# The output gate of the modulation: summed by columns during attention and spread through DRAM, instead of summed by rows late and spread by TensorE

## The chip, the cores and the metric

The kernel runs on one core of a Trainium2 chip. The metric is the device time of one execution in microseconds, and of several executions the median is taken.

## What is computed

A layer of an encoder: 512 tokens of 1024 channels, one conditioning vector `c`. Cut to what matters here:

```python
mod = jax.nn.silu(c) @ w_c[l] + b_c[l]                 # 1024 -> 3 * 1024
shift, scl, gate = jnp.split(mod, 3, axis=-1)
h = rms_norm(x, g_pre[l]) * (1.0 + scl) + shift
proj = h @ w_in[l]                                     # 1024 -> 8 * 1024
xa, za, q, k, v, zb, ga, gb = jnp.split(proj, split_pts, axis=-1)
y_a = (recurrence over xa) * silu(za) @ w_pa[l]
y_b = (neighbourhood attention of q, k, v) * silu(zb) @ w_pb[l]
merged = sigmoid(ga) * y_a + sigmoid(gb) * y_b
x = x + gate * (merged @ w_o[l])
return rms_norm(x, g_final)
```

`shift` and `scl` are needed at the start, `gate` (1024 numbers, the last third of `mod`) only near the end, where it multiplies the output of the product with `w_o`. The kernel multiplies it into the columns of `w_o` instead, so it needs `gate` as a row, the same on all 128 partitions.

## The kernel before, in words

All matrix products are made of float32 in three passes: each operand is split into a rounded part (`hi`, by ACT) and the rest (`lo`, by DVE or POOL), and TensorE adds hi*hi, hi*lo and lo*hi. A projection (`proj`, L687 on) takes one block of 128 output channels: one load of 512 KB (`wraw`), one cast on ACT (`whi`), one subtraction of 128x1024 on DVE or POOL (`wlo`), and 24 matmuls of 128x512 into a bank of PSUM (`acc`).

The stages in order: the head (parameters, norm of x, modulation), the product for v (`hx`), then four groups of attention, each for two pairs of heads. In a group TensorE makes the six projections of the next group while the attention of the last one runs between them: scores (`sp`), on DVE the bias and the minimum of each row (L821, `p`, `mn`), on ACT the exponential, on TensorE the transposes (`pt`, L835), on ACT and DVE the hi and lo part of the transposed weights (`pp`, L841 and L843), on TensorE the product with v (`pv`), and on ACT and DVE its eviction (`vp` at L860 and L863, `yt` at L866). `pv` has two banks: a next `pv` can begin when `yt` of the one before has read its bank. Then come four groups of the recurrent branch, the merge of the two branches, and the product with `w_o`, followed by the final norm.

Each step is handed to `op` with an engine, an estimated cost and a rank. A planner (`Plan`) runs a list schedule at build time from these costs and writes out one fixed order for each engine. The engines then go through their rows in that order and wait for one another by semaphores. SP issues all loads and stores but two, in one order too. An op with `lock=True` on DVE is not planned beside one on POOL.

The gate is made late, in `gate_row` (L1084 to L1121), called after the recurrent groups. Sixteen loads of 256 KB bring the rows of the gate's third of `w_c` (`wr`). DVE multiplies each by the column `silc` (the silu of c, halved, L903) and adds them up in two tiles `g`, element by element (L1095, L1097). Each of the 128 partitions then holds a part of the sum. ACT and DVE split `g` into `gh` and `gl`, and TensorE multiplies both by a matrix of ones (`onesr`), which sums over the partitions and puts the row on all of them (`mi<-gh,onesr`, `mi<-gl,onesr`). DVE adds the bias from a broadcast load (L1113) and halves (L1115). `gate[n]` multiplies the columns of `w_o` (L1155).

`shift` and `scl` are made in another way, by columns (`modulate`, L539 on): a block of `w_c` comes turned, with 128 output channels on the partitions (`wc`), and one DVE instruction multiplies it by the row `silr` (silu of c on all partitions) and sums along the row (L569).

Of the kernel before, what the change touches and what calls it, by code (L numbers as in the profile page):

```python
# [331 lines left out]
@with_exitstack  # L332
def layer(ctx, tc, x, x_t, par, w_m, w_g, bc_gate, w_v, w_in, w_blk, rpb, amask, w_pa, w_pb, w_o, g_final, out):
    nc = tc.nc
# [56 lines left out]
    def whole(t):  # L391
        return lambda: t.ap


    def const(name, shape, dt=F32):
        return pl.fixed(cp.tile(shape, dt, name=name))

    ident, onesc, onesr = const("ident", [P, P]), const("onesc", [P, P]), const("onesr", [P, P], F32R)
    prm, silc, msk, par_sb = const("prm", [P, 120]), const("silc", [P, KD]), const("msk", [P, 80]), const("par_sb", [120, P])
    tan8 = const("tan8", [8, P])  # L400
# [11 lines left out]
    pp0 = B("mi")  # L412
    op("PE", 0.25, lambda e: nc.tensor.transpose(pp0.ap[:, :120], par_sb.ap, ident.ap[:120, :120]), -20,
       r=[par_sb, ident], w=[pp0])
    op("DVE", 0.3, lambda e: nc.vector.tensor_copy(prm.ap, pp0.ap[:, :120]), -20, r=[pp0], w=[prm])
    pc = lambda a, b: prm.ap[:, a:b]
# [13 lines left out]
    for n in range(2):  # L430
        cb = B("hx")

        def f(e, n=n, cb=cb):
            for k in range(4):
                nc.tensor.matmul(cb.ap[:, k * P:(k + 1) * P], ident.ap[:120, 4 * n + k:4 * n + k + 1].to_broadcast([120, P]), par_sb.ap,
                                 start=True, stop=True)
# [96 lines left out]
    def modulate(k):  # L533

        for m, d in ((1, scs), (0, shs)):
# [4 lines left out]
            if k == 0:  # L540
# [18 lines left out]
                continue  # L559
            load(t, whole(t), w_m[2 * k + m], k - 5, 524288, spare=2, name=f"wc{k}{m}")  # L560
            if k == 1:
# [336 lines left out]
    def small(rank, after):  # L898
# [185 lines left out]
    def gate_row(pos, after):  # L1084
        op("ACT", 0.3, lambda e: nc.scalar.copy(onesr.ap, onesc.ap), pos, r=[onesc], w=[onesr], after=after)
        g = (T("g"), T("g"))
        for kk in range(KD):
            for n in range(2):
                wr = T("wr")
                load(wr, whole(wr), w_g[kk * P:(kk + 1) * P, n * 512:(n + 1) * 512], pos + 0.5 * kk, 262144,  # L1090
                     after=after, spare=12, name="wr")

                def f(e, kk=kk, n=n, wr=wr):
                    if kk == 0:
                        nc.vector.tensor_scalar(g[n].ap, wr.ap, silc.ap[:, 0:1], None, op0=ALU.mult)  # L1095
                    else:
                        nc.vector.scalar_tensor_tensor(g[n].ap, wr.ap, silc.ap[:, kk:kk + 1], g[n].ap, op0=ALU.mult, op1=ALU.add)  # L1097
                op("DVE", dve(512), f, pos + 3 + 0.5 * kk, r=[wr, silc], **({"rw": [g[n]]} if kk else {"w": [g[n]]}), lock=True,
                   name="grow")
        for n in range(2):  # L1100
            gh, gl = T("gh", F32R), T("gl", F32R)
            op("ACT", act(512), cast(whole(gh), whole(g[n])), pos + 8, r=[g[n]], w=[gh])
            op("DVE", dve(512), sub(whole(gl), whole(g[n]), whole(gh)), pos + 8, r=[g[n], gh], w=[gl], lock=True)
            o, bcg, gf = B("mi"), T("gate"), T("gfin")

            def f(e, gh=gh, gl=gl, o=o):
                mm(o.ap, onesr.ap, gh.ap, True, False)
                mm(o.ap, onesr.ap, gl.ap, False, True)
            op("PE", 0.46, f, pos + 8, r=[onesr, gh, gl], w=[o], name="grow")
            load(bcg, whole(bcg), bc_gate[n * 512:(n + 1) * 512].partition_broadcast(P), pos + 7, 262144, after=after, spare=8)  # L1110

            def f(e, o=o, bcg=bcg):
                nc.vector.tensor_tensor(bcg.ap, o.ap, bcg.ap, op=ALU.add)  # L1113

                nc.vector.tensor_scalar(bcg.ap, bcg.ap, 0.5, None, op0=ALU.mult)  # L1115
            op("DVE", dve(512) + dve2(512), f, pos + 8.2, r=[o], rw=[bcg], lock=True, name="gate")
            gate.append(bcg)
# [202 lines left out]
```

## Time and profile before

| | |
|---|---|
| median of 3 runs | 562.09 us (561.46 to 562.93) |
| the profiled execution | 561.7 us, its span 559.8 us |
| TensorE busy | 551.0 us, 98% of the span |
| DVE / ACT / POOL busy | 391.2 / 323.6 / 101.9 us |
| moved by DMA | 83.47 MB, mean 149 GB/s |

The span runs from the first to the last instruction; the execution's own time has 1.9 us more. A share of busy time tells only that TensorE is nearly always at work. Whether something is worth time is read from where TensorE waits, and for whom. Times of traces are microseconds from the start of the span.

### The profile page before, as it was taken

Reading aid. Unit: us, or ns where it says so; the run is one execution under the profiler, and the core shown is the slowest. Engines: PE = TensorE matmul, PEld = TensorE weight load, DVE = VectorE, ACT = ScalarE, POOL = GpSimd, SP = SyncE. Lnnn points to the kernel's source line nnn. Section 1 sums busy time; section 2 is a strip of 40 time slices with the busy share of each in tenths; the row PEclk is TensorE's granted clock in tenths of the full one; section 3 lists DMA queues with packets and bytes.
Section 4 is the critical chain, followed back from the end, with each engine's and each line's share of the span. In section 5 each row is a group of like instructions: output and inputs, shape, how many; then the busy total and the mean of one; then the engine's idle time right before and its main releaser. Section 6 shows DMA issues by size and latency. Waiting matters only on the chain.

```text
span 559.8 us, 7687 instructions
## 1 busy us (share of the span) xinstructions
PE 551.0 (98%) x2781; PEld 458.6 (82%) x2781; DVE 391.2 (70%) x696; ACT 323.6 (58%) x568; POOL 101.9 (18%) x95
## 2 busy tenths in 40 slices
PE   8999999999999999999999999999999999999995
PEld 8788888788888888887887888888788888888885
DVE  5999733684784876897569648866967897469523
ACT  6542623862763763787965984995698243223243
POOL 1103549555455440000000000000000000000220
PEclk9999999999999999999999999999999999999999
DMA  8993899346437434034332134032319462380002
GB/s 299 408 408 112 305 274 277 139 108 179 120 113 202 113 116 167 2 97 151 112 116 92 39 112 143 28 114 75 114 63 365 136 189 75 130 321 1 0 39 112
DMA packets 35580, 83.47 MB, mean 149 GB/s; under 512 B 3615, under 2 KB 10967, under 8 KB 35543
## 3 DMA queue, kind: packets, MB, share of 16 engines
q1 hardware_dynamic: 35264, 82.66, 44.6%
q8 instruction: 22, 0.36, 0.3%
q10 hardware_dynamic: 279, 0.32, 0.2%
q14 instruction: 15, 0.12, 0.1%
HBM read 76.65 MB, written 6.32 MB: 148 GB/s over the span
## 4 chain that ended last, share of the span: by engine, by line
PE 88%; DMA 8%; SPq 1%; DVE 1%; issue 0%; ACT 0%; POOL 0%; ACTq 0%; POOLq 0%
PE acc L384 72%; PE hx L384 8%; DMA wraw<-in_w_in_dram 3%; DMA vt<-vscr 3%; PE pv L384 3%; PE gt L384 2%; PE pt L835 2%; PE sp L384 2%; DMA wv<-in_w_v_dram 1%; DMA xT<-in_x_t_dram 1%; SPq L373 1%; SPq L678 1%; DVE va L675 0%; POOL vl L381 0%; PE mi L384 0%
## 5 line engine op out<-in xcount | busy, mean ns | idle before, releaser
L384 PE MATMUL acc<-hhl,whi 128*128 128x512 f32 x784 | 244.6, 393 | 0.0
L384 PEld LDWEIGHTS acc<-hhl,whi 128*128 128x128 f32 x784 | 143.9, 188 | 27.7
L384 PE MATMUL acc<-hhl,wlo 128*128 128x512 f32 x392 | 152.9, 390 | 0.0
L384 PEld LDWEIGHTS acc<-hhl,wlo 128*128 128x128 f32 x392 | 73.6, 188 | 15.6
L378 ACT CAST whi<-wraw 128x1024 fp32r<-128x1024 f32 x72 | 74.1, 1043 | 7.3 <-DMA wraw<-in_w_in_dram 6.6
L1186 POOL TENSOR_TENSOR yo<-yo,gfin 128x512 f32<-128x512 f32 x6 | 8.1, 1350 | 337.2 <-ACT xr L1183 337.2
L381 POOL TENSOR_TENSOR wlo<-wraw,whi 128x1024 fp32r<-128x1024 f32 x23 | 56.0, 2441 | 53.8 <-ACT whi L378 41.2
L381 DVE TENSOR_TENSOR wlo<-wraw,whi 128x1024 fp32r<-128x1024 f32 x49 | 59.2, 1220 | 9.3 <-ACT whi L378 9.1
L384 PE MATMUL acc<-woh,mhl 128*128 128x512 f32 (+1 forms) x144 | 40.4, 365 | 0.0
L384 PE MATMUL acc<-ybhl,whi 128*128 128x512 f32 x128 | 39.4, 389 | 0.0
L384 PE MATMUL acc<-yahl,whi 128*128 128x512 f32 x128 | 39.4, 389 | 0.0
L736 POOL TENSOR_TENSOR nb<-msk,braw 128x192 f32<-128x192 f32 (+1 forms) x48 | 30.7, 668 | 43.1 <-DMA braw<-in_rpb_dram 29.6
L828 ACT ACTIVATE p<-p,mn 128x192 f32<-128x192 f32 (+1 forms) x64 | 30.5, 477 | 5.8 <-DVE mn L821 5.7
L384 PE MATMUL hx<-vh,hhl 128*128 128x512 f32 x112 | 33.5, 389 | 0.0
L821 DVE CUSTOM_DVE_ANT_0 p<-sp,nb 128x192 f32<-128x192 f32 (+1 forms) x64 | 31.7, 607 | 0.9 <-PE sp L384 0.7
L1061 DVE SCALAR_TENSOR_TENSOR gm<-gm,acc 128x512 f32<-128x512 f32 x16 | 11.0, 687 | 28.6 <-PE acc L384 28.5
L384 PEld LDWEIGHTS acc<-woh,mhl 128*128 128x128 f32 x144 | 26.1, 189 | 4.4
L843 DVE TENSOR_TENSOR pp<-pt,pp 128x384 fp32r<-128x384 f32 (+1 forms) x32 | 19.8, 625 | 12.7 <-ACT pp L841 12.3
L384 PEld LDWEIGHTS acc<-yahl,whi 128*128 128x128 f32 x128 | 24.0, 188 | 5.0
L384 PEld LDWEIGHTS acc<-ybhl,whi 128*128 128x128 f32 x128 | 24.0, 188 | 5.0
L967 DVE SCALAR_TENSOR_TENSOR xc<-acc,prm,xc 128x511 f32<-128x511 f32 (+1 forms) x24 | 18.0, 749 | 12.3 <-ACT xc L960 11.7
L384 PE MATMUL acc<-wol,mhl 128*128 128x512 f32 (+1 forms) x72 | 26.3, 365 | 0.0
(202 smaller groups left out, 964.4 us busy)
## 6 DMA issues: line engine op xcount, KB each, us to landing
wraw<-in_w_in_dram SPq DMA_DIRECT2D x56, 512.0 KB
wc<-in_w_m_dram SPq DMA_DIRECT2D x14, 512.0 KB
vt<-vscr SPq DMA_DIRECT2D x24, 256.0 KB
vscr<-va SPq DMA_DIRECT2D x8, 512.0 KB
wraw<-in_w_pb_dram SPq DMA_DIRECT2D x8, 512.0 KB
wraw<-in_w_pa_dram SPq DMA_DIRECT2D x8, 512.0 KB
wr<-in_w_g_dram SPq DMA_DIRECT2D x16, 256.0 KB
wo<-in_w_o_dram SPq DMA_DIRECT2D x8, 512.0 KB
```

Of the source, the lines that this page charges most:

```text
L373: return op("SP", 0.45, lambda e: nc.sync.dma_start(dst(), src() if callable(src) else src), rank, r=r, w=[t], after=after, spare=spare, s ...
L378: return lambda e: nc.scalar.copy(o(), i()) if e == "ACT" else nc.vector.tensor_copy(o(), i())
L381: return lambda e: ENGINE[e].tensor_tensor(o(), a(), b().bitcast(F32), op=ALU.subtract)
L384: nc.tensor.matmul(o, a, b, start=first, stop=last)
L736: nc.gpsimd.tensor_tensor(o, mv, view, op=ALU.subtract)
L821: nc.vector.tensor_tensor_reduce(out=o, in0=v(spv(h, e)[:, :nk]), in1=v(nb[:, h, :nk]), scale=1.0, scalar=3e38, op0=ALU.add, op1=ALU.min, ...
L828: nc.scalar.activation(pv2(i), pv2(i), AF.Exp, bias=mn.ap[:, c:c + 1], scale=-1.0, accum_out=sm.ap[:, 2 * b + h:2 * b + h + 1])
L835: nc.tensor.transpose(ptp.ap[:, j * P:(j + 1) * P], pt_.ap[:, j * P:(j + 1) * P], ident.ap)
L843: op("DVE", dve(nt * P), lambda e_, ppv=ppv, pv4=pv4: nc.vector.tensor_tensor(ppv()[:, :, 1, :], pv4(), ppv()[:, :, 0, :].bitcast(F32), op ...
L967: nc.vector.scalar_tensor_tensor(a, b, wcol, a, op0=ALU.mult, op1=ALU.add)
L1061: op("DVE", dve(512), lambda e: nc.vector.scalar_tensor_tensor(t.ap, t.ap, 1.0, o.ap, op0=ALU.add, op1=ALU.mult), n - 1.9, r=[o], rw=[t], ...
L1186: op(("DVE", "POOL"), (dve(w), pool_(w)), lambda e: ENGINE[e].tensor_tensor(y(), y(), gfin[n].ap[:, gs], op=ALU.mult), rank + 0.1, r=[gfin ...
```

## The change

The gate is made by columns, as shift and scale are. `w_m` now holds the gate's blocks too (24 instead of 16), already turned. Eight loads of 512 KB (`wc`) are put between the projections' loads during the first two groups of attention, and after each of them one DVE instruction of 128x1024 (L954, operation `ISA`) multiplies by `silr`, sums along the row, adds the bias and leaves 128 of the gate's numbers in one column of `gcol`. The bias comes from 8 further rows of the parameter table `par` (128 rows instead of 120). After the eighth, DVE halves the columns and turns `gcol` (128x32) in pieces of 32 by 32 (`STREAM_TRANSPOSE`, L960). One DMA on SP writes the result to DRAM (`gscr`, L962) so that the gate lies there as a row. In `gate_row` two broadcast loads bring it to all partitions. The sixteen loads, the sums, the split, the four matmuls and the additions of the old way are gone, and so is `silc` in the head.

```diff
+GR = 17
...
-    ident, onesc, onesr = const("ident", [P, P]), const("onesc", [P, P]), const("onesr", [P, P], F32R)
-    prm, silc, msk, par_sb = const("prm", [P, 120]), const("silc", [P, KD]), const("msk", [P, 80]), const("par_sb", [120, P])
+    ident, onesc = const("ident", [P, P]), const("onesc", [P, P])
+    prm, msk, par_sb = const("prm", [P, P]), const("msk", [P, 80]), const("par_sb", [P, P])
...
+    def turned(scr):
+
+        return bass.AP(scr.tensor, scr.offset, [[32, 4], [P, 32], [1, 32]])
...
-        op("DVE", 0.2, lambda e: nc.vector.tensor_scalar(silc.ap, pc(0, 8), 0.5, None, op0=ALU.mult), rank, r=[prm], w=[silc])
...
+    gcol, gtur = const("gcol", [P, 32]), T("gtur")
+    gscr = pl.fixed(dp.tile([32, P], F32, name="gscr"))
+    op("POOL", 0.1, lambda e: nc.gpsimd.memset(gcol.ap, 0.0), 8, w=[gcol])
+    for k in range(KD):
+        t, r = W("wc"), gcol.part()
+        load(t, whole(t), w_m[3 * k + 2], GR + k, 524288, after=[main[GR + k - 2]], spare=6, name=f"wc{k}2")
+        op("DVE", dve(1024) + 0.08, lambda e, k=k, t=t: nc.vector.tensor_tensor_reduce(
+            out=t.ap, in0=t.ap, in1=silr.ap, scale=0.5, scalar=pc(120 + k, 121 + k), op0=ALU.mult, op1=ALU.add,
+            accum_out=gcol.ap[:, k:k + 1]), GR + 3 + k, r=[silr, prm], rw=[t], w=[r], lock=True, name="gate")
+
+    def turn(e):
+        nc.vector.tensor_scalar(gcol.ap[:, :8], gcol.ap[:, :8], 0.5, None, op0=ALU.mult)
+        nc.vector.transpose(gtur.ap[:, :32], gcol.ap)
+    op("DVE", 0.35, turn, GR + 12, rw=[gcol], w=[gtur], name="gturn")
+    op("SP", 0.5, lambda e: nc.sync.dma_start(turned(gscr.ap), gtur.ap[:, :32]), GR + 12, r=[gtur], w=[gscr], size=16384, late=SLACK, name="gscr")
...
     def gate_row(pos, after):
-        op("ACT", 0.3, lambda e: nc.scalar.copy(onesr.ap, onesc.ap), pos, r=[onesc], w=[onesr], after=after)
-        g = (T("g"), T("g"))
-        for kk in range(KD):
-            for n in range(2):
-                wr = T("wr")
-                load(wr, whole(wr), w_g[kk * P:(kk + 1) * P, n * 512:(n + 1) * 512], pos + 0.5 * kk, 262144,
-                     after=after, spare=12, name="wr")
...
         for n in range(2):
-            gh, gl = T("gh", F32R), T("gl", F32R)
...
-                mm(o.ap, onesr.ap, gh.ap, True, False)
-                mm(o.ap, onesr.ap, gl.ap, False, True)
...
+            bcg, gf = T("gate"), T("gfin")
+            load(bcg, whole(bcg), bass.AP(gscr.ap.tensor, gscr.ap.offset + n * 512, [[0, P], [1, 512]]), pos + 7, 262144, r=[gscr],
+                 after=after, spare=8)
             gate.append(bcg)
```

Since the planner makes its order anew, the change also moves other rows. The order of SP and of TensorE in the head and in the product for v is as before, but for the shape of one transpose. In the first two groups of attention the rows of all engines stand in another order; from the third group on they are as before, up to the merge.

The first place is the row in which TensorE made the gate, at the end of a merge projection. Before (`yahl` is the recurrent branch, `hhl` the normed input):

```order
L384 MATMUL acc_4597<-hhl_547,whi_4465 128x512 x2
L384 MATMUL acc_4597<-hhl_547,wlo_4471 128x512
L384 MATMUL mi_4638<-gh_4620,onesr 128x512
L384 MATMUL mi_4638<-gl_4631,onesr 128x512
L384 MATMUL acc_4597<-hhl_587,whi_4465 128x512 x2
L384 MATMUL acc_4597<-hhl_587,wlo_4471 128x512
L384 MATMUL mi_4646<-gh_4626,onesr 128x512
L384 MATMUL mi_4646<-gl_4636,onesr 128x512
L384 MATMUL acc_4653<-yahl_3386,whi_4514 128x512 x2
L384 MATMUL acc_4653<-yahl_3386,wlo_4536 128x512
```

and now:

```order
L385 MATMUL acc_4576<-hhl_547,wlo_4479 128x512
L385 MATMUL acc_4576<-hhl_587,whi_4470 128x512 x2
L385 MATMUL acc_4576<-hhl_587,wlo_4479 128x512
L385 MATMUL acc_4612<-yahl_3414,whi_4511 128x512 x2
L385 MATMUL acc_4612<-yahl_3414,wlo_4523 128x512
```

The four matmuls of `mi` are gone; the projections on both sides of them stand as before.

The second place is DVE in the first group of attention, near the end of the pair's work, where the third product `pv` and the fourth are evicted. Before:

```order
L843 TENSOR_TENSOR pp_1237<-pt_1226,pp_1237 128x3x128
L843 TENSOR_TENSOR pp_1275<-pt_1261,pp_1275 128x4x128
L877 RECIPROCAL rc_1295<-sm_1112 128x8
L863 TENSOR_TENSOR vp_1269<-pv_1252,vp_1269 64x256
L863 TENSOR_TENSOR vp_1269<-pv_1283,vp_1269 64x256
L866 TENSOR_TENSOR yt_1312<-pv_1252,vp_1269 64x2x128
L889 TENSOR_TENSOR sz_830<-sz_830,rcx_1259 128x512
L891 TENSOR_TENSOR sz_830<-yt_1155,sz_830 128x512
L875 SCALAR_TENSOR_TENSOR sz_1310<-sz_1310,acc_1216 128x512
L866 TENSOR_TENSOR yt_1312<-pv_1283,vp_1269 64x2x128
L843 TENSOR_TENSOR pp_1323<-pt_1305,pp_1323 128x4x128
L381 TENSOR_TENSOR ybhl_1339<-sz_830,ybhl_1339 128x512
```

and now, with two of the eight gate reductions (`gcol`):

```order
L848 TENSOR_TENSOR pp_1255<-pt_1243,pp_1255 128x3x128
L882 RECIPROCAL rc_1283<-sm_1114 128x8
L848 TENSOR_TENSOR pp_1261<-pt_1208,pp_1261 128x4x128
L954 ISA wc_1145,gcol<-wc_1145,silr_160,prm 128x1024
L954 ISA gcol 128x1
L868 TENSOR_TENSOR vp_1298<-pv_1276,vp_1298 64x256
L868 TENSOR_TENSOR vp_1298<-pv_1293,vp_1298 64x256
L871 TENSOR_TENSOR yt_1323<-pv_1276,vp_1298 64x2x128
L871 TENSOR_TENSOR yt_1323<-pv_1293,vp_1298 64x2x128
L848 TENSOR_TENSOR pp_1316<-pt_1302,pp_1316 128x4x128
L954 ISA wc_1240,gcol<-wc_1240,silr_160,prm 128x1024
L954 ISA gcol 128x1
```

A gate reduction stands between the lo part of the transposed weights (`pp_1261`) and the eviction (`vp_1298`) of the two `pv` before; another stands before the products with the reciprocals (`sz`, the next three rows). The `yt` of the second bank, which stood behind the three `sz`, now stands before them.

The third place is TensorE beside it. Before, from the end of the second `pv` of the pair:

```order
L384 MATMUL pv_1283<-pp_1237,vt_756 128x256
L384 MATMUL acc_1216<-hhl_547,whi_929 128x512 x2
L384 MATMUL acc_1216<-hhl_547,wlo_960 128x512
L384 MATMUL acc_1216<-hhl_587,whi_929 128x512 x2
L384 MATMUL acc_1216<-hhl_587,wlo_960 128x512
L882 MATMUL mi_1303<-ident,rc_1295 8x128
L835 MATMUL pt_1305<-ident,p_1257 128x128 x4
L384 MATMUL acc_1314<-hh_281,whi_1044 128x512
L384 MATMUL acc_1314<-hl_296,whi_1044 128x512
L384 MATMUL acc_1314<-hh_281,wlo_1085 128x512
L384 MATMUL acc_1314<-hhl_343,whi_1044 128x512 x2
L384 MATMUL acc_1314<-hhl_343,wlo_1085 128x512
```

and now, from the end of the answering `pv` to the beginning of the next:

```order
L385 MATMUL pv_1293<-pp_1255,vt_756 128x256
L887 MATMUL mi_1300<-ident,rc_1283 8x128
L840 MATMUL pt_1302<-ident,p_1204 128x128 x4
L385 MATMUL acc_1232<-hhl_547,whi_929 128x512 x2
L385 MATMUL acc_1232<-hhl_547,wlo_960 128x512
L385 MATMUL acc_1232<-hhl_587,whi_929 128x512 x2
L385 MATMUL acc_1232<-hhl_587,wlo_960 128x512
L385 MATMUL acc_1325<-hh_281,whi_1046 128x512
L385 MATMUL acc_1325<-hl_296,whi_1046 128x512
L385 MATMUL acc_1325<-hh_281,wlo_1087 128x512
L385 MATMUL pv_1337<-pp_1261,vt_770 128x256
```

Before, the next product `pv_1348` came after 21 matmuls of `acc`, a transpose of `rc` (`mi`) and four of `p`; now `pv_1337` comes after nine matmuls, the transpose of `rc` and four of `p`. It writes a bank that `yt_1323` must have read.

## Rows read from the trace of the kernel before

**Rows 1.** The page: busy time of the engines, share of the span, instructions.

```profile
PE 551.0 (98%) x2781; PEld 458.6 (82%) x2781; DVE 391.2 (70%) x696; ACT 323.6 (58%) x568; POOL 101.9 (18%) x95
```

**Rows 2.** Waits of TensorE and of its weight loads after the head (window from 16.8 us): engine, line, whom it waited for, us in total, times, longest.

```profile
PE pv L384 <- DVE pp L843: 0.4, 1, 0.4
PE hx L384 <- POOL vl L381: 0.2, 1, 0.2
```

**Rows 3.** Busy time by stretches: the stretch, its length, busy us (and instructions) of PE, PEld, DVE, ACT, POOL, granted clock, DMA share, GB/s. The first is the head, the second all until TensorE's last matmul, the third the tail; then the first group of attention (two rows), the second (two rows), the last recurrent group and the merge.

```profile
0.00:16.87 16.87, 14.93 (x107) 14.15 (x107) 10.34 (x33) 10.39 (x21) 3.21 (x11) 1.00 0.89 318
16.87:553.44 536.57, 536.10 (x2674) 444.49 (x2674) 378.60 (x656) 312.20 (x546) 98.68 (x84) 1.00 0.44 144
553.44:559.80 6.36, 0.00 (x0) 0.00 (x0) 2.31 (x8) 1.02 (x2) 0.00 (x0) 0.91 0.32 125
101.23:124.25 23.02, 23.02 (x129) 19.52 (x130) 18.71 (x43) 17.60 (x49) 12.24 (x11) 1.00 0.33 101
124.25:137.19 12.94, 12.94 (x59) 10.42 (x58) 6.22 (x10) 4.23 (x7) 7.77 (x6) 1.00 0.82 221
137.19:167.51 30.32, 30.32 (x199) 26.02 (x199) 23.61 (x61) 21.37 (x58) 15.34 (x15) 1.00 0.38 106
167.51:180.46 12.95, 12.95 (x60) 10.43 (x58) 6.22 (x10) 4.23 (x7) 7.78 (x6) 1.00 0.78 221
396.59:440.00 43.41, 43.41 (x203) 35.64 (x204) 34.69 (x44) 35.25 (x48) 0.00 (x0) 1.00 0.54 188
440.00:471.47 31.47, 31.47 (x140) 26.06 (x139) 26.57 (x39) 9.75 (x14) 0.00 (x0) 1.00 0.34 110
```

**Rows 4.** The chain of work that ended last, around the gate's matmuls and at the end: start, us, what.

```profile
469.85 0.46 PE mi L384 x2
470.31 0.70 PE acc L384 x3
471.02 0.46 PE mi L384 x2
471.47 81.95 PE acc L384 x384
```

**Rows 5.** DVE by line and shape, whole span: name, shapes, count, busy us, mean ns of one, idle before. First what goes, then the instruction that makes shift (the one most like the new one) with its read of the sum, and two small ones.

```profile
L1097 DVE SCALAR_TENSOR_TENSOR g<-wr,silc,g 128x512 f32<-128x512 f32 x14 | 9.9, 746 | 0.0
L1095 DVE TENSOR_SCALAR g<-wr,silc 128x512 f32<-128x512 f32 x2 | 0.9, 479 | 0.0
L381 DVE TENSOR_TENSOR gl<-g,gh 128x512 fp32r<-128x512 f32 x2 | 1.3, 683 | 0.0
L1113 DVE TENSOR_TENSOR gate<-mi,gate 128x512 f32<-128x512 f32 x2 | 1.4, 684 | 0.0
L1115 DVE TENSOR_SCALAR gate<-gate 128x512 f32<-128x512 f32 x2 | 0.9, 428 | 0.1
L569 DVE CUSTOM_DVE_ANT_0 wc<-wc,silr,prm 128x1024 f32<-128x1024 f32 x6 | 7.7, 1277 | 0.0
L569 DVE DVE_READ_ACCUMULATOR2_ANT sh<- 128x1 f32 x6 | 0.5, 80 | 0.0
L903 DVE TENSOR_SCALAR silc<-prm 128x8 f32<-128x8 f32 x1 | 0.2, 164 | 0.0
L415 DVE COPY prm<-mi 128x120 f32<-128x120 f32 x1 | 0.3, 283 | 0.6 <-PE mi L413 0.6
```

**Rows 6.** The head in order of time, two rows of POOL: start, us, line, what, idle before.

```profile
1.40 0.10 POOL L450 MEMSET epsc<- 128x1 f32 x1
15.54 1.28 POOL L381 TENSOR_TENSOR vl<-wv,vh 128x512 fp32r<-128x512 f32 x1 [12.90 <-ACT vh L378]
```

**Rows 7.** DMA issues: name, queue, count, KB each.

```profile
wr<-in_w_g_dram SPq DMA_DIRECT2D x16, 256.0 KB
wc<-in_w_m_dram SPq DMA_DIRECT2D x14, 512.0 KB
```

**Rows 8.** Waits of SP's queue, and of ACT's casts of weights after 101.23 us (the only one with `whi` in that window).

```profile
SPq L885 <- ACT rct L883: 65.2, 8, 21.3
...
ACT whi L378 <- PE acc L384: 0.4, 1, 0.4
```

**Rows 9.** DVE and POOL in order of time, in the first group of attention: two DVE instructions that meet a `wlo` of POOL, and the same two kinds without one.

```profile
119.16 0.67 DVE L889 TENSOR_TENSOR sz<-sz,rcx 128x512 f32<-128x512 f32 x1
122.24 2.30 DVE L381 TENSOR_TENSOR ybhl<-sz,ybhl 128x512 fp32r<-128x512 f32 x1
127.58 1.38 DVE L889 TENSOR_TENSOR sz<-sz,rcx 128x512 f32<-128x512 f32 x1
133.03 0.68 DVE L381 TENSOR_TENSOR ybhl<-sz,ybhl 128x512 fp32r<-128x512 f32 x1
...
121.58 2.40 POOL L381 TENSOR_TENSOR wlo<-wraw,whi 128x1024 fp32r<-128x1024 f32 x1 [2.97 <-ACT whi L378]
126.01 2.40 POOL L381 TENSOR_TENSOR wlo<-wraw,whi 128x1024 fp32r<-128x1024 f32 x1 [0.87 <-POOL vt L756]
```

**Rows 10.** Durations used for the narrow place: TensorE from the chain (four matmuls of `pv`, four transposes `pt`, six of `acc`), ACT and DVE evictions in order of time.

```profile
115.62 0.44 PE pt L835 x4
116.06 1.39 PE acc L384 x6
117.45 0.47 PE pv L384 x4
...
117.96 0.37 ACT L860 COPY vp<-pv 64x256 f32<-64x256 f32 x1 [0.29 <-PE pv L384]
...
113.34 0.86 DVE L863 TENSOR_TENSOR vp<-pv,vp 64x256 f32<-64x256 f32 x2
114.24 0.88 DVE L866 TENSOR_TENSOR yt<-pv,vp 64x256 f32<-64x256 f32 x2
```

More of the change, by code (lines that the diff above doesn't have):

```diff
@@ L332, in layer @@
 @with_exitstack
-def layer(ctx, tc, x, x_t, par, w_m, w_g, bc_gate, w_v, w_in, w_blk, rpb, amask, w_pa, w_pb, w_o, g_final, out):
+def layer(ctx, tc, x, x_t, par, w_m, w_v, w_in, w_blk, rpb, amask, w_pa, w_pb, w_o, g_final, out):
     nc = tc.nc
@@ L412, in layer @@
     pp0 = B("mi")
-    op("PE", 0.25, lambda e: nc.tensor.transpose(pp0.ap[:, :120], par_sb.ap, ident.ap[:120, :120]), -20,
+    op("PE", 0.25, lambda e: nc.tensor.transpose(pp0.ap[:, :P], par_sb.ap, ident.ap), -20,
        r=[par_sb, ident], w=[pp0])
-    op("DVE", 0.3, lambda e: nc.vector.tensor_copy(prm.ap, pp0.ap[:, :120]), -20, r=[pp0], w=[prm])
+    op("DVE", 0.3, lambda e: nc.vector.tensor_copy(prm.ap, pp0.ap[:, :P]), -20, r=[pp0], w=[prm])
     pc = lambda a, b: prm.ap[:, a:b]
@@ L434, in f @@
             for k in range(4):
-                nc.tensor.matmul(cb.ap[:, k * P:(k + 1) * P], ident.ap[:120, 4 * n + k:4 * n + k + 1].to_broadcast([120, P]), par_sb.ap,
+                nc.tensor.matmul(cb.ap[:, k * P:(k + 1) * P], ident.ap[:, 4 * n + k:4 * n + k + 1].to_broadcast([P, P]), par_sb.ap,
                                  start=True, stop=True)
@@ L559, in modulate @@
                 continue
-            load(t, whole(t), w_m[2 * k + m], k - 5, 524288, spare=2, name=f"wc{k}{m}")
+            load(t, whole(t), w_m[3 * k + m], k - 5, 524288, spare=2, name=f"wc{k}{m}")
             if k == 1:
@@ L1084, in gate_row @@
     def gate_row(pos, after):
-        op("ACT", 0.3, lambda e: nc.scalar.copy(onesr.ap, onesc.ap), pos, r=[onesc], w=[onesr], after=after)
-        g = (T("g"), T("g"))
-        for kk in range(KD):
-            for n in range(2):
-                wr = T("wr")
-                load(wr, whole(wr), w_g[kk * P:(kk + 1) * P, n * 512:(n + 1) * 512], pos + 0.5 * kk, 262144,
-                     after=after, spare=12, name="wr")
[L1093 to L1099, printed above, removed]
-        for n in range(2):
-            gh, gl = T("gh", F32R), T("gl", F32R)
[L1102 to L1106, printed above, removed]
-                mm(o.ap, onesr.ap, gh.ap, True, False)
-                mm(o.ap, onesr.ap, gl.ap, False, True)
[L1109 to L1116, printed above, removed]
+        for n in range(2):
+            bcg, gf = T("gate"), T("gfin")
+            load(bcg, whole(bcg), bass.AP(gscr.ap.tensor, gscr.ap.offset + n * 512, [[0, P], [1, 512]]), pos + 7, 262144, r=[gscr],
+                 after=after, spare=8)
             gate.append(bcg)
@@ L1281 @@
     w_in = a["w_in"].reshape(D, 8 * D)
-    mod = a["w_c"].reshape(D, 3, KD, P)[:, :2].transpose(2, 1, 3, 0).copy()
+    mod = a["w_c"].reshape(D, 3, KD, P).transpose(2, 1, 3, 0).copy()
     mod[0, 1] = tiles(a["w_c"].reshape(D, 3 * D)[:, D:D + P])[0]
@@ L1287 @@
         f("c"), f("g_pre"), f("b_c")[:2 * D], f("conv_w"), f("conv_b"),
-        f("b_r_f"), swap(f("b_i_f")), f("b_r_b"), swap(f("b_i_b")), f("lam_f"), f("lam_b"),
-    ]).reshape(120, P)
+        f("b_r_f"), swap(f("b_i_f")), f("b_r_b"), swap(f("b_i_b")), f("lam_f"), f("lam_b"), f("b_c")[2 * D:],
+    ]).reshape(P, P)
     pad = np.zeros((1, PAD), np.float32)
@@ L1295 @@
         "par": par,
-        "w_m": mod.reshape(2 * KD, P, D),
-        "w_g": a["w_c"].reshape(D, 3 * D)[:, 2 * D:],
-        "bc_gate": f("b_c")[2 * D:].copy(),
+        "w_m": mod.reshape(3 * KD, P, D),
         "w_v": w_in[:, 4 * D:5 * D].reshape(KD, P, D),
```

## The prediction

> **What bounds the kernel now.** I read the shares first: TensorE is busy 98% of the span, DVE 70% [rows 1]. A share does not say who sets the end, so the stretches come next: TensorE's first dense matmul stands at 16.87 us and its last ends at 553.44 us, and in these 536.57 us it is busy for 536.10 [rows 3]. What is left over is in the waits of TensorE: one of 0.4 us for the lo part of a transposed weight (`pp`, at 101.23 us in the first group of attention) and one of 0.2 at the very start [rows 2]. The granted clock is 1.00 in all of these stretches, so no clock is to be won either [rows 3]. The span is therefore a head of 16.87 us, a solid row of matmuls, and a tail of 6.36 us. To change the time one must take matmuls out of the row, change head or tail, or make TensorE wait.
>
> **The change, part by part.**
>
> *Matmuls of the old gate.* They lie in the solid row: two pairs of 0.46 us, each between matmuls that run on without a gap [rows 4]. Three `acc` matmuls beside them take 0.70 [rows 4], or 0.93 for four, the same size. They go: 0.92 us off the path. No other matmul is added or taken away; one transpose in the head has 128 columns instead of 120.
>
> *DVE, what goes.* 14 x 0.746 + 2 x 0.479 + 2 x 0.683 + 2 x 0.684 + 2 x 0.428 = 10.4 + 1.0 + 1.4 + 1.4 + 0.9 = 15.0 us [rows 5], in the last recurrent group and the merge, where DVE is busy 34.7 of 43.4 and 26.6 of 31.5 us [rows 3]. TensorE waits for DVE nowhere there [rows 2], so this gives nothing: the work lay beside matmuls. The casts that go on ACT likewise.
>
> *DVE, what comes.* The new reduction is the one that makes shift: 1.277 us and 0.080 for the read of its sum [rows 5], 8 x 1.357 = 10.9 us. Halving the columns and the turn of 128x32 are not in the trace; between the small instruction of 128x8, 0.16, and the copy of 128x120, 0.28 [rows 5], each, so 0.3 to 0.6 for both, and I take 0.4, since both are nearer to the small one in width. All of it comes in the first two groups of attention, 101.23 to 180.46 us, where DVE is busy 18.71 + 6.22 + 23.61 + 6.22 = 54.8 of 79.2 us [rows 3]. It would be 66.1 of 79.2. On average that fits; whether it fits at each place is the question of this change.
>
> *The narrow place.* In the first group the new order has, after the second `pv` of a pair, `mi`, four transposes and nine `acc` matmuls before the next `pv`. With four transposes at 0.44 and six `acc` at 1.39 [rows 10] this is 0.11 + 0.44 + 1.5 x 1.39 = 2.64 us; 0.11 is a quarter of the transposes' 0.44. Before, 21 `acc` lay there, 4.86 + 0.55 = 5.4 us. In this time ACT copies from the bank and DVE does two `vp` and two `yt`. Counted from the end of the second `pv`: the gate reduction stands ahead of them. The instruction ahead of it, `pp_1261`, ends some 0.7 us before my zero if DVE takes up its rows as soon as their inputs are there (an estimate from the same durations), so the reduction ends near 0.6; then `vp` 0.86 and `yt` 0.88 [rows 10] end at 2.35, and TensorE comes at 2.64. The margin is 0.3 us. In the second group a like place (the reduction before `ql` and the eviction, then `rc`) has a margin I put at 0.0 to 0.5 by the same count. Elsewhere I find 1 us or more.
>
> *What may stretch a reduction.* With no `wlo` of POOL beside them the two kinds of DVE instruction took 0.67 and 0.68 us; with one they took 1.38 and 2.30, and each ended about 0.55 us after the `wlo`: 128.96 against 128.41, and 124.54 against 123.98 [rows 9]. So DVE stood until POOL was done. A reduction that meets a `wlo` of 2.40 us is late by up to 2.4. POOL is busy 12.24 + 7.77 + 15.34 + 7.78 = 43.1 of the 79.2 us [rows 3], so of eight reductions some four would meet POOL if they fell at random; they do not quite, since the planner keeps them apart by its costs.
>
> *The price for TensorE.* From below: nothing, and the 0.44 of the wait that is there may even go. From above: all eight reductions on the path, 10.9 us. The nearest row is the wait that this same stage has now, 0.4 once in four groups made by the same planner with the same costs [rows 2]. I take one more wait of that size, 0.4.
>
> *Loads.* 16 x 256 KB go and 8 x 512 KB come [rows 7]: 4 MB either way. They move from the merge to the first two groups, where the DMA share is 0.33 to 0.82 [rows 3], 4 MB more in 79 us being 53 GB/s. The two broadcasts of the bias become two of the gate. Nothing of this is waited for: after 101.23 us no cast of weights on ACT waited for a load [rows 8]. The cover is that the loads run several projections ahead. If it went, a cast would be late by what the load is late.
>
> *SP's queue.* The store of the turned gate waits for DVE, and behind it on SP stand the next weights, the store of the reciprocals and the biases. SP stands like this already, eight times for the reciprocals, 65.2 us in all and up to 21.3 at once, without a late cast [rows 8]. One more such wait, of the size of DVE's lateness, costs nothing.
>
> *The head.* `silc` (0.16, [rows 5]) goes from DVE, which then waits for squares anyway; the clearing of `gcol` on POOL, about the 0.10 of a small memset, comes where POOL later stands idle for 12.90 us [rows 6]. Eight more rows of parameters, no price seen. Nothing, to within 0.2 us either way. The tail's instructions are the same.
>
> **The sum.** The profiled execution took 561.7 us, 0.4 below the median of 562.09. 561.7 - 0.92 + 0.4 = 561.2 for it, and with the 0.4 to the median **561.6 us**. A measurement of this kernel can tell about 0.3%, 1.7 us, from no change, so this is no change: the gate was nearly all hidden and stays so.
>
> **The rivals.**
>
> *B, slower: reductions lose the race against POOL at both narrow places.* The mechanism is that of the two stretched instructions [rows 9]. It decides as soon as a `wlo` begins before the reduction: then DVE starts after it, up to 2.4 late, and beyond the margin of 0.3 TensorE waits 2.1. At two places 4.2: 562.1 - 0.9 + 4.2 = 565.4. For it: the cast that releases a `wlo` stands on ACT just before the copies from the bank, so the two begin within a few tenths of one another. Against it: TensorE's wait in this stage is 0.4 now, though DVE is 81% busy at 101 to 124 us [rows 3], so the plan holds on the chip. The Trainium skill, page SBUF — State Buffer, section SBUF: two separate sides, says that VectorE with two SBUF inputs and a GpSimd instruction that reads SBUF exclude one another for a whole instruction, whoever comes first. By that rule, with the trace agreeing (2.30 against 0.68), each of the eight reductions is open to this, as both of its inputs lie in SBUF. Chance 0.12. With one place lost: 562.1 - 0.9 + 2.1 = 563.3, chance 0.12, still within 0.3%.
>
> *C, faster: the relief counts.* The wait of 0.4 at 101 us goes with the new order, and head and tail come out 0.4 shorter by chance of the loads: 562.1 - 0.9 - 0.4 - 0.4 = 560.4. Against it: the order of TensorE before that wait is unchanged. That the 15.0 us of DVE show is excluded by the rows, since nobody waits for DVE there. Chance 0.06.
>
> *D, the change does not hide the store.* If DVE's turn came a group late, 43.3 us (137.19 to 180.46 [rows 3]), SP would stand, the weights behind it would come late by that less what they are ahead, and TensorE would stop for several us: about 567. The eight waits of SP speak against it [rows 8]. Chance 0.02.
>
> **How the numbers follow.** My forecast has 0.68, one place lost 0.12, both lost 0.12, C 0.06, D 0.02. Faster by over 0.3% (below 560.4): half of C and a little of the forecast's lower edge, 0.05. Slower (above 563.8): B, D and the upper edge of the case of one place, 0.15. The same: 0.80. The range goes down to 560.5, the bare 561.2 of the median without any new wait less the 0.4 that could go and 0.3 of head, and up to 563.8, which takes in one place lost with the wait of 0.4 besides; it leaves out C's lower half, B and D, under 2 in 10.
>
> **What would show it.** Right: no `mi<-gh` rows, TensorE busy about 535.2 us between the head's end and its last matmul, that stretch 535.6 to 536.5 long, a sum of TensorE's waits on DVE under 1 us, and DVE at some 387 us in all. The reduction should show near 1.28 us where POOL is idle and up to 3.7 beside a `wlo`. Wrong: waits of TensorE on `pp` or on the eviction `yt` of more than 2 us, with a stretched reduction just before them on DVE; or a cast of weights waiting for its load behind the store of the gate; or a head that is not 16.9 us long.

## The result and the profile after

| | before | after |
|---|---|---|
| first comparison, 21 runs each | 562.12 us (560.92 to 564.85) | 565.16 us (561.85 to 566.92), ratio 1.0046 [1.0033, 1.0059] |
| the profiled execution | 561.7 us, span 559.8 | 562.25 us, span 560.5 |
| three later comparisons of the same two kernels, on three chips | 562.95, 563.08, 563.54 us | 562.98, 563.03, 563.65 us |
| ratios there, 12 runs of after each | | 1.0008 [0.9983, 1.0033], 1.0005 [0.9985, 1.0025], 1.0013 [0.9986, 1.0039] |

A ratio stands with its 95% interval. The first comparison says slower by 0.46%. The other three find no difference (0.05% to 0.13%, intervals up to 0.4%). So the interval of one comparison does not take in what differs between comparisons. Both kernels spread by 2.5 to 6.6 us from run to run, and the profiled execution of the changed kernel is among the fastest two of its 21. So there are two questions: what the change itself costs, which the traces answer, and what spreads the runs, which took the experiments.

Busy time after, beside [rows 1]: TensorE has the four matmuls less, and DVE, forecast 4 us lower, is 2 us higher.

```profile
PE 550.9 (98%) x2777; PEld 458.2 (82%) x2777; DVE 393.0 (70%) x691; ACT 322.4 (58%) x565; POOL 103.1 (18%) x96
```

The three stretches, beside [rows 3]. The dense one is 536.56 us long against 536.57, though four matmuls are gone from it:

```profile
0.00:17.39 17.39, 15.38 (x107) 14.50 (x107) 10.57 (x32) 10.43 (x21) 3.27 (x12) 1.00 0.86 314
17.39:553.95 536.56, 535.55 (x2670) 443.65 (x2670) 380.13 (x653) 310.92 (x543) 99.79 (x84) 1.00 0.44 144
553.95:560.50 6.55, 0.00 (x0) 0.00 (x0) 2.31 (x8) 1.02 (x2) 0.00 (x0) 0.89 0.32 121
```

Waits of TensorE after the head, beside [rows 2]:

```profile
PE pv L385 <- DVE pp L848: 0.8, 1, 0.8
PE hx L385 <- POOL vl L382: 0.2, 1, 0.2
```

DVE by line and shape: the eight reductions, their reads, the turn and the halving, as [rows 5]. The mean of a reduction is 1742 ns, not 1280: five of the eight took 1.28 us, the others 1.67, 2.61 and 3.27.

```profile
L954 DVE CUSTOM_DVE_ANT_0 wc<-wc,silr,prm 128x1024 f32<-128x1024 f32 x8 | 13.9, 1742 | 0.0
L954 DVE DVE_READ_ACCUMULATOR2_ANT gcol<- 128x1 f32 x8 | 0.6, 80 | 0.0
L960 DVE STREAM_TRANSPOSE gtur<-gcol 128x32 f32<-128x32 f32 x1 | 0.2, 211 | 0.0
L959 DVE TENSOR_SCALAR gcol<-gcol 128x8 f32<-128x8 f32 x1 | 0.1, 114 | 0.0
```

The narrow place in order of time, all engines, chosen rows:

```profile
116.54 0.64 DVE L848 TENSOR_TENSOR pp<-pt,pp 128x512 fp32r<-128x512 f32 x1
116.89 2.39 POOL L382 TENSOR_TENSOR wlo<-wraw,whi 128x1024 fp32r<-128x1024 f32 x1 [3.37 <-ACT whi L379]
117.09 3.27 DVE L954 CUSTOM_DVE_ANT_0 wc<-wc,silr,prm 128x1024 f32<-128x1024 f32 x1
...
120.30 0.86 DVE L868 TENSOR_TENSOR vp<-pv,vp 64x256 f32<-64x256 f32 x2
...
120.47 2.38 POOL L382 TENSOR_TENSOR wlo<-wraw,whi 128x1024 fp32r<-128x1024 f32 x1 [1.20 <-PE acc L385]
120.70 0.64 PE L385 MATMUL pv<-pp,vt 128*128 128x256 f32 x4
121.19 0.88 DVE L871 TENSOR_TENSOR yt<-pv,vp 64x256 f32<-64x256 f32 x2
...
122.10 0.69 DVE L848 TENSOR_TENSOR pp<-pt,pp 128x512 fp32r<-128x512 f32 x1
...
122.85 0.74 PE L385 MATMUL pv<-pp,vt 128*128 128x256 f32 x4 [0.82 <-DVE pp L848]
```

Read it from the top. POOL begins `wlo` 0.2 us before DVE comes to the reduction, and the reduction ends at 120.36, 1.08 us after the `wlo`. DVE is 2 us late; `vp`, `yt` and then `pp` follow it, and the *second* `pv` after it, which needs this `pp`, waits 0.82. The first, at 120.70, does not wait, although `yt` has not begun. The Trainium skill, page SBUF — State Buffer, section SBUF: two separate sides, has these two instructions exclude one another; the trace agrees (3.27 us against 1.28).

What it costs in all is read from landmarks that no wait hides: the time from the first `pv` of the first group to the first `sp` of the next two groups, and from the first `acc<-yahl` to the first matmul of the product with `w_o`. The rows of before:

```profile
101.23 0.75 PE L384 MATMUL pv<-pp,vt 128*128 128x256 f32 x4 [0.44 <-DVE pp L843]
137.12 0.36 PE L384 MATMUL sp<-kh,qh 64*128 64x192 f32 x2
180.39 0.36 PE L384 MATMUL sp<-kh,qh 64*128 64x192 f32 x2
437.72 0.62 PE L384 MATMUL acc<-yahl,whi 128*128 128x512 f32 x2
509.42 0.39 PE L384 MATMUL acc<-woh,mhl 128*128 128x512 f32 x1
```

and of after:

```profile
101.47 0.74 PE L385 MATMUL pv<-pp,vt 128*128 128x256 f32 x4
138.51 0.36 PE L385 MATMUL sp<-kh,qh 64*128 64x192 f32 x2
181.88 0.36 PE L385 MATMUL sp<-kh,qh 64*128 64x192 f32 x2
439.20 0.61 PE L385 MATMUL acc<-yahl,whi 128*128 128x512 f32 x2
509.92 0.39 PE L385 MATMUL acc<-woh,mhl 128*128 128x512 f32 x1
```

The merge: 71.70 against 70.72, so 0.98 won. The two groups: 79.16 against 80.41, so 1.25 lost, 1.15 of it before the second group. So the change costs 0.27 us by these two traces. Two more traces of the changed kernel (e1 and g4, below) have the same 80.41 and 70.72, each to 0.01. That is no 3 us.

### The profile page after: what moved, and what is told of

It is laid out like the page before. It is cut to its first block, busy times and chain, and to the rows that moved or that the text cites. A ratio compares the mean times of both kernels' runs of the same rounds, so it can differ in the third digit from the quotient of the medians.

```text
span 560.5 us, 7664 instructions
## 1 busy us (share of the span) xinstructions
PE 550.9 (98%) x2777; PEld 458.2 (82%) x2777; DVE 393.0 (70%) x691; ACT 322.4 (58%) x565; POOL 103.1 (18%) x96
## 4 chain that ended last, share of the span: by engine, by line
PE 88%; DMA 7%; DVE 2%; SPq 2%; issue 1%; ACT 0%; POOL 0%; ACTq 0%; DVEq 0%
PE acc L385 71%; PE hx L385 8%; DMA vt<-vscr 3%; PE pv L385 3%; PE gt L385 2%; PE pt L840 2%; SPq L374 2%; PE sp L385 2%; DMA wraw<-in_w_in_dram 1%; DMA wv<-in_w_v_dram 1%; DMA xT<-in_x_t_dram 1%; DVE wc L954 1%; DVE pp L848 0%; DVE yt L871 0%; DVE vp L868 0%
```

## The experiments

All were timed in five rounds, 12 runs each, beside the kernel before. Theory after these traces: the 0.82 us is the collision with POOL, and the rest of the slowdown comes from elsewhere. Rivals: the new order, the loads, the head.

**e1, the changed kernel again.** 

> The changed kernel once more, for the trace of a usual run: its profiled execution took 562.25 us, but the median of 21 is 565.16. All theories expect 564.5 to 566 and a ratio of 1.004 to 1.006. Theory K (collision: a gate reduction, with both inputs in SBUF, stands until a wlo of POOL is done, and TensorE waits behind it at the narrow places; a wait long enough lowers the granted clock after it): waits of TensorE on pp or yt of 1 to 3 us in the first two groups, a stretched L954 of over 3 us just before, and a stretch with a granted clock under 1.00 behind them. Theory L (loads of wc get in the way): waits that end with a DMA.

Measured: 562.98 us (561.71 to 568.31), ratio 1.0008, which none of the theories had expected. The wait of 0.82 is there again (at 123.75 us), behind a reduction of 3.27 us. A second wait of 1.54 us stands at the first `pv` of the first group, at 102.37 us, where the profiled execution before had 0.44 [rows 2] and the one after none. So this wait is not a fixed one.

**e2, reductions that read one input.**

```diff
-        op("DVE", dve(1024) + 0.08, lambda e, k=k, t=t: nc.vector.tensor_tensor_reduce(
-            out=t.ap, in0=t.ap, in1=silr.ap, ...
+        op("DVE", dve(1024) + 0.08, lambda e, k=k, t=t: nc.vector.tensor_reduce(
+            out=gcol.ap[:, k:k + 1], in_=t.ap, op=ALU.add, axis=mybir.AxisListType.X),
```

The product with the silu and the bias are left out. 

> The eight gate reductions are replaced, in the same places of the same order, by a plain sum over the same 128x1024 with one input (the gate's numbers are then wrong; everything else is as in the changed kernel). About the same time on DVE, 1.1 to 1.3 us each, but only one operand from SBUF. Theory K: they no longer stand behind POOL, no L954 over 1.5 us, and the time falls to 561.2 to 562 (before less 0.9, with at most the old wait). Theory O (the new order itself has too little room) and theory L: 565 as before. Theory D (DVE is simply too full in these two groups): 564.5 to 565.5.

Measured: 561.23 us, ratio 0.9979 [0.9961, 0.9996]. The same place, POOL and then DVE:

```profile
116.11 2.39 POOL L382 TENSOR_TENSOR wlo<-wraw,whi 128x1024 fp32r<-128x1024 f32 x1 [3.35 <-ACT whi L379]
```

```profile
116.30 1.21 DVE L954 TENSOR_REDUCE gcol<-wc 128x1 f32<-128x1024 f32 x1
117.43 0.88 DVE L868 TENSOR_TENSOR vp<-pv,vp 64x256 f32<-64x256 f32 x2
118.34 0.88 DVE L871 TENSOR_TENSOR yt<-pv,vp 64x256 f32<-64x256 f32 x2
119.25 0.69 DVE L848 TENSOR_TENSOR pp<-pt,pp 128x512 fp32r<-128x512 f32 x1
```

The `wlo` begins 0.2 us ahead as before, and the reduction is not held up; `pv` does not wait. The one-input form also writes no row of 128x1024 back, so this edit alone does not tell the second input from the write. Other rows do. In the trace after the next `wlo`, from 120.47 to 122.85 us, runs beside `vp` and `yt`, which read one input from PSUM and one from SBUF and write to SBUF; they take 0.86 and 0.88 us, as at 114.15 and 115.05 us, where POOL is idle. `sz` and `ybhl`, the same operation with both inputs in SBUF, were held up [rows 9]. So it is the second input in SBUF that makes the collision.

**e3, the order and the loads without the sums.**

```diff
-        op("DVE", dve(1024) + 0.08, lambda e, k=k, t=t: nc.vector.tensor_tensor_reduce(...), GR + 3 + k, ...
+        op("DVE", dve(1024) + 0.08, lambda e: None, GR + 3 + k, ...
```

The gate is not summed. 

> The order of the changed kernel with its eight loads, but the eight reductions are left out (the gate is then wrong). Theories K and D: 560.8 to 561.6, the 0.9 of the four matmuls and no new wait. Theories O and L: 564 to 565.5, since order and loads are the same.

Measured: 561.69 us, ratio 0.9988 [0.9973, 1.0003]. Its trace is the yardstick, since TensorE's order is that of the changed kernel:

```profile
103.27 0.75 PE L385 MATMUL pv<-pp,vt 128*128 128x256 f32 x4 [2.48 <-DVE pp L848]
139.22 0.36 PE L385 MATMUL sp<-kh,qh 64*128 64x192 f32 x2
182.46 0.36 PE L385 MATMUL sp<-kh,qh 64*128 64x192 f32 x2
```

From `pv` to the two `sp` it takes 35.95 and 79.19 us, before 35.89 and 79.16, after 37.04 and 80.41. So the new order costs nothing, and the sums cost 1.09 in the first group and 0.13 in the second, 1.22 in all. (The view counts the wait of 0.82 from the end of the matmul before it. That matmul begins at 121.64 and the `pv` 1.21 us later, where matmuls of the solid row begin 0.23 apart; so most of the 1.09 is this wait.) But here the first `pv` waits 2.48 us, with no sum anywhere. ACT shows why:

```profile
95.82 0.19 ACT L833 ACTIVATION_READ_ACCUMULATOR p<-p,mn 128x1 f32 x1
101.21 1.04 ACT L379 CAST whi<-wraw 128x1024 fp32r<-128x1024 f32 x1 [5.20 <-DMA wraw<-in_w_in_dram]
102.16 0.47 ACT L846 CAST pp<-pt 128x384 fp32r<-128x384 f32 x1
```

The copy `pp`, which the first `pv` needs, stands on ACT behind a cast of weights, and that waits for its load. In the kernel before it is the same row:

```profile
99.16 1.05 ACT L378 CAST whi<-wraw 128x1024 fp32r<-128x1024 f32 x1 [3.14 <-DMA wraw<-in_w_in_dram]
```

e1, e2 and e3 have the same order up to this place and ran on the same chip; their first waits are 1.54, 0.18 and 2.48 us.

**e4, loads and reductions put into the recurrent groups**, where POOL is idle (`GR = 36`, the block moved behind that loop). 

> The same gate by columns, turned and through DRAM, but its loads and reductions are placed 19 projections later, in the first two recurrent groups, where POOL has nothing to do; the order of the attention groups is then that of the kernel before. Theory K: 561.2 (the kernel before less 0.92), each reduction near 1.28 us, no new wait. Theory D for the later place, where DVE is busy 70 to 80%: up to 563. Theories O and L say the same as K here, as the order and the loads of the first two groups are the old ones.

Measured: 560.95 us (559.67 to 564.82), ratio 0.9971 [0.9951, 0.9991], faster than both kernels. All eight reductions took 1.28 us:

```profile
L1092 DVE CUSTOM_DVE_ANT_0 wc<-wc,silr,prm 128x1024 f32<-128x1024 f32 x8 | 10.2, 1278 | 0.0
```

**f1, f3, f4: a cast moved on ACT.** These three were to move the cast that waits. By mistake of the edit (a `late=6.0` for one projection's load) the cast of the projection ahead of it moved, one row, so they test nothing of what they were for; they count as further draws. 

> The changed kernel with one cast of weights (ACT, first group of attention, the one at about 99 to 101 us that waits for its load) moved two rows back on ACT, behind the copy `pp` and the exponentials beside it; every other row of every engine stands as before. Theory 1 (two separate waits: the first `pv` of the first group waits because `pp` stands on ACT behind a cast that waits for its load, 0 to 2.5 us from run to run; the later `pv` at 122.85 us waits 0.8 us because a gate reduction is held up by POOL): the first wait is 0, the second stays at 0.8, median about 561.5, 1 to 1.5 us below the changed kernel, and the runs spread less. Rival (the spread of the runs is the clock or the chip and not this wait): median 562.5 to 565 as the changed kernel, spread 4 us or more.

 

> The kernel of e4 (gate loads and reductions in the recurrent groups) with the same cast moved two rows back on ACT. Theory 1: TensorE has no wait on `pp` of over 0.1 us, median about 560.4, 0.3 to 1 us below that of e4 (560.95), fewer runs over 562. Rival (the spread is the clock or the chip): median and spread as e4, 560.9 with runs up to 564.

 

> The kernel before with the same cast moved two rows back on ACT, all other rows as they were. Theory 1: its wait of 0.44 us at 101 us goes, and so do the longer ones that other runs have: 0.4 to 1 us faster than the kernel before, ratio 0.998 to 0.9995, spread smaller than 4 us. Rival (the spread is the clock or the chip): ratio 1.000, spread as in the kernel before.

Measured: 562.51, 561.65 and 562.03 us, beside 563.24 for the kernel before. First waits 2.08, 1.80 and 0. In f1 the granted clock (last but two of each row) falls behind the wait:

```profile
100.00:102.00 2.00, 0.56 (x3) 0.13 (x1) 0.00 (x0) 1.43 (x3) 0.31 (x1) 1.00 0.87 308
102.00:104.00 2.00, 1.36 (x8) 1.36 (x9) 1.97 (x8) 1.98 (x9) 2.00 (x1) 0.77 1.02 288
104.00:106.00 2.00, 2.00 (x9) 1.60 (x8) 1.17 (x5) 1.18 (x4) 0.07 (x1) 0.50 0.70 227
106.00:108.00 2.00, 2.00 (x11) 1.69 (x10) 0.84 (x2) 1.41 (x3) 0.00 (x0) 0.87 0.21 82
108.00:110.00 2.00, 2.00 (x12) 1.67 (x11) 2.00 (x4) 1.89 (x6) 0.00 (x0) 1.00 0.03 12
```

0.50 is the lower of the two levels, 1.2 GHz. From `pv` to the next `sp` f1 takes 38.47 us against 37.04: the fall costs 1.4 us on top of the wait of 2.1.

**f2, the first gate load later**: SP issues it at about 100 us with the second, all else as in the changed kernel. 

> The changed kernel with SP issuing the first gate load (512 KB) not at about 95 us, behind the three loads of weights, but at about 100 us together with the second; all other rows as in the changed kernel. Theory 2 (the early gate load shares the DMA engines with the load of weights that the cast at 99 to 101 us waits for, and so the change itself makes the first wait longer): the first wait is 0.5 us at most, the wait at 122.85 us stays at 0.8, median about 561.8, 1 us or more below the changed kernel. Theory 1 (that load comes late in any case, behind the eight loads of v that fill the DMA engines): the first wait varies as in the changed kernel, median the same within 0.5 us.

Measured: 563.76 us, ratio 1.0032 [1.0008, 1.0056], first wait 1.66. Without the early load the wait is as long as with it: theory 2 is not borne out. The later load has a price of its own here: the first reduction waits 0.79 us for it (at 107.64 us), and from `pv` to the next `sp` it takes 37.60 us, not 37.04.

**g1, g2, g3: now the right cast behind `pp`** and the four exponentials, in the changed kernel, in e4 and in the kernel before; **g4, the changed kernel again**. The planner keeps its order, and the writing of the row is held back:

```diff
         self.log.append(o)
-        o.fn(e)
+        held = self.__dict__.setdefault("held", [])
+        if o.name in ("whi18", "wlo18") and (held or o.name == "whi18"):
+            held.append((o, e))
+        else:
+            o.fn(e)
+            if e == "ACT" and held:
+                self.passed = self.__dict__.get("passed", 0) + 1
+                while held and self.passed == 5:
+                    h, f = held.pop(0)
+                    h.fn(f)
```

> The changed kernel with ACT's cast `whi` that waits for its load at 99 to 101 us put behind the copy `pp` and the four exponentials that followed it; all other rows of all engines unchanged. (In f1, f3 and f4 the row that was moved was the cast one earlier, so they did not test this.) Theory 1 (two waits: the first `pv` of the first group hangs on this load through ACT's order and varies from run to run, 0 to 2.5 us, with a fall of the clock behind the longest; the `pv` at 122 us waits 0.8 for the reduction held up by POOL): the first `pv` waits under 0.3 us however late the load lands, the wait of 0.8 at 122 us stays, granted clock 1.00 at 100 to 110 us, median about 561.8, few runs over 563.5. Rival (the spread comes from the head or the chip): median and spread as the changed kernel beside it.

 

> The kernel of e4 (gate loads and reductions in the recurrent groups) with the same row of ACT put behind `pp` and the exponentials. Theory 1: no wait of TensorE on `pp` over 0.3 us, median about 560.5, ratio to the kernel before 0.996 to 0.998, few runs over 562.5. Rival: as e4, ratio 0.997 with runs up to 564.

 

> The kernel before with the same row of ACT put behind `pp` and the exponentials. Theory 1: first wait gone, median 0.5 to 1.2 us below the kernel before, and within 0.3 us of g1, since the change then stands at -0.92 for the four matmuls and +0.82 for the wait at 122 us. Rival: ratio 1.000 to the kernel before, spread as before.

 

> The changed kernel, unchanged, a third time. Theory 1: between 562.5 and 565, 0.7 us or more above g1, with a first wait anywhere from 0 to 2.5 us and the wait of 0.8 at about 122 us. Rival (the slowdown of the first chip is a property of the change): 565 again, ratio 1.004 or more.

| | median | lowest to highest | ratio to before |
|---|---|---|---|
| before, 35 runs | 563.08 | 560.93 to 567.49 | |
| g4, changed | 563.03 | 562.20 to 564.70 | 1.0005 [0.9985, 1.0025] |
| g3, before, `pp` first | 560.94 | 560.44 to 561.44 | 0.9956 [0.9936, 0.9977] |
| g1, changed, `pp` first | 561.30 | 560.75 to 562.63 | 0.9975 [0.9959, 0.9991] |
| g2, e4, `pp` first | 560.06 | 559.08 to 560.72 | 0.9948 [0.9933, 0.9963] |

One row of ACT takes 2.1 us off the kernel before and brings its spread from 6.6 us (35 runs) to 1.0 (12 runs). ACT in g1: the load lands later still (101.91), and the `pv` at 100.99 waits for nothing:

```profile
98.42 0.48 ACT L855 CAST pp<-pt 128x384 fp32r<-128x384 f32 x1 [2.06 <-PE pt L849]
...
101.91 1.05 ACT L388 CAST whi<-wraw 128x1024 fp32r<-128x1024 f32 x1 [1.14 <-DMA wraw<-in_w_in_dram]
```

With the spread mostly gone the change can be read from medians: +0.36 us (g1 less g3), and -0.88 (g2 less g3) where the reductions meet no POOL. Drawing the twelve runs of each at random again and again puts these between 0.0 and 0.9 and between -1.2 and -0.5 (an estimate). The traces gave +0.27, and -0.98 for the matmuls alone.

The price of the change is not the same in every run, though. The profiled execution of g1 is the slowest of its twelve, and its two groups take 81.31 us against 78.94 in g3: 2.37 lost, not 1.25. The wait of 0.82 is there at 123.26, and a further 0.28 at 109.92, behind a copy `pp` that the late cast held back and a reduction that itself waited for its load:

```profile
106.55 1.28 DVE L963 CUSTOM_DVE_ANT_0 wc<-wc,silr,prm 128x1024 f32<-128x1024 f32 x1 [0.46 <-DMA wc<-in_w_m_dram]
```

**h1, h2, h3: does the change lengthen the first wait?** h1 adds an idle load of 512 KB to the kernel before where the first gate load goes; h2 leaves out the gate loads of the changed kernel (its reductions multiply the silu row by itself, so the gate is not computed); h3 is the changed kernel once more. 

> The kernel before with one load of 512 KB added (into a buffer that nobody reads), issued by SP where the changed kernel issues its first gate load, behind the three loads of weights at about 91 to 94 us; every other row unchanged. Theory 2 (an early gate load delays the landing of the weights that the cast at 99 to 101 us waits for): the first `pv` waits 1 us or more, median 0.5 to 1.5 us above the kernel before. Theory 1 (that wait is set by when the loads of v start, from run to run, and not by the gate load): median within 0.4 us of the kernel before.

 

> The changed kernel with the eight gate loads left out; the reductions read the row of the silu twice, so the gate is not the layer's. Theory 1: the wait of 0.8 at about 122 us stays (the reduction still reads two inputs in SBUF beside POOL), the first wait varies, median 562 to 563. Theory 2: first wait 0 to 0.3, median 561.5 to 562.

 

> The changed kernel, unchanged, on one more chip. Theory 1: median between 562 and 564, within 0.5 us of the kernel before. Rival (the first chip's +3.0 us belongs to the change): 564.5 or more, ratio 1.004 or more.

Measured beside 563.54 us for the kernel before: 562.20 (ratio 0.9984 [0.9961, 1.0008]), 563.60 (1.0009) and 563.65 (1.0013). First waits 1.94, 1.14 and 2.34. The load added does not slow the median, the loads taken away do not speed it up: theory 2 is not borne out. The kernel before with one idle load shows the fall of the clock too (h1, same columns):

```profile
102.00:104.00 2.00, 1.22 (x7) 1.22 (x8) 1.84 (x6) 2.00 (x9) 2.00 (x1) 0.78 0.88 266
104.00:106.00 2.00, 2.00 (x8) 1.60 (x7) 1.30 (x5) 1.29 (x5) 0.20 (x1) 0.50 0.29 110
```

## Why the prediction was wrong, by its steps

*Matmuls of the old gate, -0.92.* Right: 0.98 measured.

*What goes from DVE is worth nothing.* Right: TensorE waits for DVE nowhere in the recurrent groups and the merge.

*What comes, 10.9 + 0.4 us.* The single prices held (1.28, 0.08; 0.33 for the halving and the turn), the sum did not: 14.6 + 0.3, since three reductions stood beside POOL.

*The narrow place.* The place and the collision were right. The waiter was not: I let the next `pv` wait for `yt`, since I took it to write a bank that `yt_1323` must have read (so says the section on the change, too). It began at 120.70 us and `yt` at 121.19, so this was not so; the `pv` after it waits, for `pp`. So more work lay between, and 2.0 us of lateness became 0.82 of waiting, not 2.1. In the second place it became 0.13.

*The price for TensorE: "I take one more wait of that size, 0.4".* This is the step of the sum that failed by size. It is 1.22. I had drawn 0.4 from a wait of another kind: the 0.44 at 101 us belongs to a load, not to DVE's crowding. With 0.98 and 1.22 the sum is 561.7 + 0.24 + 0.4 = 562.3, no change, and inside the range. So this error alone does not explain the 565.16 of the first comparison.

*The 0.44 itself, taken as the same in each run.* As far as is known, this step took the median of the first comparison out of the range of 560.5 to 563.8. [rows 8] begins at 101.23 us; the cast that makes this wait stands at 99.16 and waited 3.14 us for its load. "no cast of weights on ACT waited for a load" held because the window began 2 us too late. In the profiled executions of this study the wait was anywhere from 0 to 2.48 us (in the four of the changed kernel itself 0, 1.54, 1.52 and 2.34), and three times the clock fell behind it, for 1.4 to 1.5 us more (f1, h1, h3). g3 shows that this wait makes nearly all of the spread of the kernel before, g1 and g2 that without it no run reaches 563 us. Some 3.5 us between a lucky run and an unlucky one is ten times what the change does.

*Loads, SP's queue.* Right for the median: h1 and h2 find no price for the loads. "Nothing of this is waited for" does not hold for every run: in g1 and f2 a reduction waited 0.46 and 0.79 for its load, and TensorE lost time behind it. The rest held: the store of the gate is issued at 164 us and the broadcasts at 418, and no cast waits behind them.

*The head, 16.9 to within 0.2.* Too narrow: 17.39 here, 16.5 to 17.2 in the other profiles of this study. (The granted clock is not 1.00 in all stretches of [rows 3]: the tail has 0.91. No matmul stands there, so nothing hangs on it.)

*The rivals.* B had the mechanism, and 1.22 is what came of it, in place of 2.1 or 4.2. That B's 565.4 lies beside the 565.16 of the first comparison is chance. C did not come: the wait at 101 us did not go with the new order (1.5 us or more in three of the four traces), and the head of the profile after is longer, not shorter. Nor did D: the store of the gate held nothing up. The 0.92 of the matmuls shows in full once the collision is moved away: g2 is faster than g3 by 0.88.

**What stays open.** In the first comparison 16 of 21 runs of the changed kernel took over 564.3 us and one of 21 of the kernel before; in the three later ones it was 2, 2 and 5 of 12, and before 8, 10 and 9 of 35, 35 and 29. Runs of that length are what a first wait of 2 us with the clock's fall gives, and h3 has such a trace (565.59 us). That the clock fell in the first comparison is on record: of each run the mean granted clock of the span is known. It was 0.993 to 0.995 in ten of the 21 runs of the changed kernel, all of 565.16 us or more, and 0.996 or more in the other eleven. The profiled executions with the fall (f1, h1, h3) have 0.995, all others 0.996 or more, and so has every run of g1, g2 and g3. That a first wait stood ahead of the fall in those ten runs is inferred: no trace of them exists. Why the changed kernel met it so much more often there was not found; on the chips of f2, h1 and h2 neither the early load nor the loads together bring it about, and the chip of the first comparison is not known.

## What to carry to other kernels

Before a wait is priced, follow it back to what it ends on, and look past the edge of the window: a wait that ends on a load can differ from run to run, as here, and one profile shows one draw of it. An in-order engine should not have a cast that waits for a load ahead of a copy that TensorE needs; here that one row was worth more than the change. New work on DVE with two inputs in SBUF belongs where POOL is idle, even if DVE is busier there.

## What the runs showed of the hardware

A one-input `TENSOR_REDUCE` of 128x1024 took 1.21 us beside a `wlo` that had begun 0.2 us earlier, where the two-input form took 3.27. A stall of TensorE of 1.9 to 2.3 us was followed by a granted clock of 0.50 for some 3 us in f1, h1 and h3, but one of 2.48 in e3 was not: there the clock stayed at 1.00. What tells them apart was not found.
